# A hybrid encoder trunk on one core: ten up projections of the gated MLP by seven products, and the sums for them formed a block ahead

## The chip, the cores and the metric

The kernel runs on one core of a Trainium2 chip. Its engines are TensorE (PE in the profile, with PEld for its weight loads), VectorE (DVE), ScalarE (ACT), GpSimd (POOL) and SyncE (SP, which here only issues transfers). The metric is the device time of one execution in microseconds. The profile comes from one execution, and its durations are those of that execution.

## The reference, cut to what matters

The trunk has two layers over 512 tokens of width 1024. Each layer mixes tokens (differential attention in layer 0, gated linear attention in layer 1, cross-attention beside both) and then runs a gated MLP with a causal convolution of width 3. Only the MLP is touched by the change:

```python
D_MODEL, SEQ, DEPTH, D_FF, CONV_WIDTH = 1024, 512, 2, 2816, 3

def conv_ffn(h, w_up, conv_w, conv_b, w_down):
    u = h @ w_up                       # 512 x 1024 by 1024 x 5632
    c = lax.conv_general_dilated(u, conv_w[:, None, :], window_strides=(1,),
                                 padding=[(CONV_WIDTH - 1, 0)],
                                 dimension_numbers=('NWC', 'WIO', 'NWC'),
                                 feature_group_count=u.shape[-1]) + conv_b
    a, g = jnp.split(c, 2, axis=-1)
    return (jax.nn.silu(g) * a) @ w_down   # 512 x 2816 by 2816 x 1024

for i in range(DEPTH):
    ...
    h = rms_norm(x, ffn_norm[i])
    x = x + conv_ffn(h, w_up[i], conv_w[i], conv_b[i], w_down[i])
```

## The kernel before

**Products.** Everything is computed transposed: features on the 128 partitions, the 512 tokens along a row. fp32 factors are split into a high and a low part (`fp32r`), and each product is three matmuls: high by high, high by low, low by high. Weights arrive in blocks of 1024 columns (`raw`, three buffers, all on SP's queue); ACT casts a block to `whi` and DVE subtracts to get `wlo` (`split_weights`, L254 to L258; six buffers each, `WB`). The tokens' parts are `xsh` and `xsl`, one pair of tiles for each of the eight K tiles of 128.

**The MLP** is `ffn`. The 22 feature tiles of `D_FF` are done in three passes of 4, 4 and 3 groups q of 256 features (`HALVES`: q = 0 to 3, 4 to 7, 8 to 10). For each q there are two *up pieces*, `ua` (linear half) and `ug` (gate half), each with 256 columns of `w_up` in two blocks. A piece gives two PSUM banks of 128 x 512, n = 0 and 1, each by 24 matmuls of 512 columns (`up`, `product`, L387 to L389). The order on TensorE is written out by hand: ua n=0, ug n=0, ua n=1, ug n=1. Banks go round the eight of `TURNS`. After each bank, `conv` scales it on DVE (L1165), ACT writes the first tap into `cvo` (L1167), and DVE adds the two shifted taps (L1168, L1169). ACT applies Silu to the gate half (L1333), DVE multiplies (L1334), and `parts_of` splits the result into the tiles `mid` (L1190 on ACT, L1191 on DVE).

**Down by seven products.** After the up pieces of a pass come four *down pieces* of 256 output columns. Most (`dn`) already use a scheme of Strassen's kind: for a pair of K tiles, 2 x 2 blocks of weights times 2 x 2 blocks of data (tokens 0 to 255 are `left`, 256 to 511 `right`) cost seven products of 256 columns instead of eight. For that POOL forms four sums of each weight block's quarters (`combined`, L287 to L290, tile `wsum`), and four sums of each pair of `mid` tiles are formed by `combine` (L1198 to L1201, tile `tsum`; on POOL, but on DVE for a pass's last q). TensorE's rows are then L1247, and `decode` puts the seven results together (L1258 to L1266). Layer 0's last pass (`dw`) is plain: of each two columns, the first two groups q = 8 and 9 come first for both, q = 10 after that.

**What sets the order.** TensorE runs in program order. DVE, ACT and POOL run the order that a scheduler made from the program, each then strictly in turn. `weights` decides how far ahead blocks are split; `ahead` issues the next raw loads. Down, `refill` and `release` count the split blocks that are live (a `dn` block takes two of the six buffers).

## Time and profile before

| what | value |
|---|---|
| median of three runs | 1149.71 us (1149.57 to 1151.2) |
| the profiled execution | 1150.36 us |
| its span, first to last instruction | 1148.5 us |
| matmuls of layer 0's MLP, up of pass 1, 2, 3 begin | about 241, 368.50, 495.88 us |
| down of pass 1, 2, 3 begins | 328.19, 455.57, 561.20 us |
| layer 1's, up of pass 2 and 3 begins | 920.23, 1047.61 us |

Times in the views count from the span's start. A row of a group view names line, engine, operation, result and sources and the shape, with its count; then the busy time, the mean of one in ns, and the idle time ahead of it with what ended it. A row of the timeline starts with start and duration. A row of a table of stretches starts with the stretch and its length, and has the busy time and the count of PE, PEld, DVE, ACT and POOL, then the granted clock, the share of the transfer engines and GB/s. A row of the chain has the start, the time, and the engine with what it worked on.

### The profile page before, as it was taken

Reading aid. Unit: us, or ns where it says so; the run is one execution under the profiler, and the core shown is the slowest. Engines: PE = TensorE matmul, PEld = TensorE weight load, DVE = VectorE, ACT = ScalarE, POOL = GpSimd, SP = SyncE. Lnnn points to the kernel's source line nnn. Section 1 sums busy time; section 2 is a strip of 40 time slices with the busy share of each in tenths; the row PEclk is TensorE's granted clock in tenths of the full one; section 3 lists DMA queues with packets and bytes.
Section 4 is the critical chain, followed back from the end, with each engine's and each line's share of the span. In section 5 each row is a group of like instructions: output and inputs, shape, how many; then the busy total and the mean of one; then the engine's idle time right before and its main releaser. Section 6 shows DMA issues by size and latency. Waiting matters only on the chain.

```text
span 1148.5 us, 16655 instructions
## 1 busy us (share of the span) xinstructions
PE 1142.7 (99%) x6311; PEld 985.1 (86%) x6311; DVE 871.2 (76%) x1455; ACT 592.0 (52%) x1032; POOL 193.2 (17%) x230
## 2 busy tenths in 40 slices
PE   9999999999999999999999999999999999999998
PEld 7888888888899888988888888988888988899887
DVE  8576778688789677977677637777887977797777
ACT  6676686555454354434457634535644444453442
POOL 0000000001543125500000000000135403360340
PEclk9999999999999999999999999999999999999999
DMA  9522242133214322343252220333241342234212
GB/s 293 173 83 84 78 142 74 58 109 110 92 57 146 111 77 80 96 144 100 69 182 70 100 94 12 101 125 119 74 126 40 127 149 74 61 91 143 92 46 102
DMA packets 39662, 117.83 MB, mean 103 GB/s; under 512 B 4767, under 2 KB 7256, under 8 KB 39582
## 3 DMA queue, kind: packets, MB, share of 16 engines
q1 hardware_dynamic: 39150, 116.37, 31.8%
q8 instruction: 50, 0.82, 0.3%
q10 hardware_dynamic: 432, 0.39, 0.1%
q14 instruction: 30, 0.25, 0.1%
HBM read 112.54 MB, written 4.21 MB: 102 GB/s over the span
## 4 chain that ended last, share of the span: by engine, by line
PE 99%; DMA 0%; DVE 0%; ACT 0%; issue 0%
PE ps_mm L365 6%; PE ps_mm L367 6%; PE ps_mm L366 6%; PE ps_mm L387 6%; PE ps_mm L388 6%; PE ps_mm L389 6%; PE ps_lg L1247 5%; PE ps_sm L388 5%; PE ps_sm L389 5%; PE ps_sm L387 5%; PE ps_mm L1247 4%; PE ps_tp L388 4%; PE ps_lg L388 4%; PE ps_tp L387 4%; PE ps_lg L387 4%; PE ps_tp L389 4%
## 5 line engine op out<-in xcount | busy, mean ns | idle before, releaser
L258 DVE TENSOR_TENSOR wlo<-raw,whi 128x1024 fp32r<-128x1024 f32 (+4 forms) x174 | 194.2, 1127 | 77.0 <-ACT whi L255 76.4
L255 ACT CAST whi<-raw 128x1024 fp32r<-128x1024 f32 (+4 forms) x174 | 168.0, 976 | 124.2 <-PE ps_sm L388 29.8
L365 PE MATMUL ps_mm<-whi,xsh 128*128 128x512 f32 (+2 forms) x328 | 126.2, 385 | 0.0
L367 PE MATMUL ps_mm<-whi,xsl 128*128 128x512 f32 (+2 forms) x328 | 123.0, 375 | 0.0
L366 PE MATMUL ps_mm<-wlo,xsh 128*128 128x512 f32 (+2 forms) x328 | 122.8, 374 | 0.0
L387 PE MATMUL ps_mm<-xsh,whi 128*128 128x512 f32 x278 | 109.3, 393 | 0.0
L388 PE MATMUL ps_mm<-xsl,whi 128*128 128x512 f32 x278 | 108.4, 390 | 0.0
L389 PE MATMUL ps_mm<-xsh,wlo 128*128 128x512 f32 x278 | 108.2, 389 | 0.0
L387 PE MATMUL ps_sm<-xsh,whi 128*128 128x512 f32 x218 | 84.8, 389 | 0.0
L388 PE MATMUL ps_sm<-xsl,whi 128*128 128x512 f32 x218 | 84.8, 389 | 0.0
L389 PE MATMUL ps_sm<-xsh,wlo 128*128 128x512 f32 x218 | 84.8, 389 | 0.0
L365 PEld LDWEIGHTS ps_mm<-whi,xsh 128*128 128x128 f32 x328 | 61.7, 188 | 11.4 <-issue 1.0
L367 PEld LDWEIGHTS ps_mm<-whi,xsl 128*128 128x128 f32 x328 | 61.7, 188 | 11.3
L366 PEld LDWEIGHTS ps_mm<-wlo,xsh 128*128 128x128 f32 x328 | 61.8, 188 | 10.1
L387 PE MATMUL ps_lg<-xsh,whi 128*128 128x512 f32 x160 | 62.2, 389 | 0.0
L388 PE MATMUL ps_lg<-xsl,whi 128*128 128x512 f32 x160 | 62.2, 389 | 0.0
L389 PE MATMUL ps_lg<-xsh,wlo 128*128 128x512 f32 x160 | 62.2, 389 | 0.0
L387 PE MATMUL ps_tp<-xsh,whi 128*128 128x512 f32 x160 | 62.2, 389 | 0.0
L388 PE MATMUL ps_tp<-xsl,whi 128*128 128x512 f32 x160 | 62.2, 389 | 0.0
L389 PE MATMUL ps_tp<-xsh,wlo 128*128 128x512 f32 x160 | 62.2, 389 | 0.0
L389 PEld LDWEIGHTS ps_mm<-xsh,wlo 128*128 128x128 f32 x278 | 52.2, 188 | 11.0
L387 PEld LDWEIGHTS ps_mm<-xsh,whi 128*128 128x128 f32 x278 | 52.2, 188 | 10.8 <-issue 0.3
(382 smaller groups left out, 2835.4 us busy)
## 6 DMA issues: line engine op xcount, KB each, us to landing
raw<-in_wpack_dram SPq DMA_DIRECT2D x178, 512.0 KB, 3.5
xt<-in_x_t_dram SPq DMA_DIRECT2D x15, 256.0 KB, 5.2
raw<-in_wpack_dram SPq DMA_DIRECT2D x15, 256.0 KB, 3.1
raw<-in_wpack_dram SPq DMA_DIRECT2D x8, 384.0 KB, 3.0
xres<-xt SPq DMA_DIRECT2D x8, 256.0 KB, 3.2
xt<-xres SPq DMA_DIRECT2D x8, 256.0 KB, 5.8
out_dram<-xt SPq DMA_DIRECT2D x7, 256.0 KB, 2.0
bt<-bias_d SPq DMA_DIRECT2D x6, 256.0 KB, 4.1
```

The costliest lines, as they stand in the source:

```text
L255: ins = A.copy(hi[:, c], raw[:, c])
L258: V.tensor_sub(lo[:, c], raw[:, c], hi[:, c].bitcast(F32))
L365: mm(p, sh[k][:, blk(b)], hi, start=k == 0, stop=False)
L366: mm(p, sh[k][:, blk(b)], lo, start=False, stop=False)
L367: mm(p, sl[k][:, blk(b)], hi, start=False, stop=k == KT - 1)
L387: mm(p, hi[:, blk(n)], bh, start=i == first, stop=False)
L388: mm(p, hi[:, blk(n)], bl, start=False, stop=False)
L389: mm(p, lo[:, blk(n)], bh, start=False, stop=i == last)
L1247: mm(banks[c][b][:, h], w, v, start=b not in seen[c], stop=m == nq - 1 and t == 2 and i in close)
```

## The change

Ten up pieces, the list `SEVEN`, go over to seven products: `ua` of q = 5, 6, 8 and 9 in both layers, and in layer 0 also `ug` of q = 9 and `ua` of q = 10. Such a piece takes its K tiles in the order 6, 7, 4, 5, 0, 1, 2, 3. The pair (6, 7) stays plain, 12 matmuls of 512 columns; each other pair becomes 21 of 256 (`up_by_seven`). The piece holds four banks and gives both n at once, so both stand ahead of the gate half; one ACT copy and six DVE additions put them together before `conv`.

The tokens' side needs four sums for each of the three pairs, formed once a layer in pass 1 (`token_sums`, at `SUMS_AT`): ACT scales two tiles, POOL makes four sums, ACT and DVE split them into `vsh` and `vsl`. The weights' side needs `block_sums` on POOL for each block, of 128 columns for the first block of a piece and 256 for the second.

The sums of a block are now put down when the block is next to be split (in `ahead`), before the other work that comes between, and POOL keeps the program's order. POOL's sums of `mid` use the same tile `wsum` (two buffers), `tsum` is gone, and their splitting is put behind the third convolution that follows (`later`, `behind`). DVE's sums of `mid` use `cvo` tiles. `begin`, `refill` and `release` now count live blocks in the up products too, and up and down take banks from one round of `TURNS`. The program is built with a smaller scratch for descriptors.

```diff
-                piece(("ua", l, q), "w_up", l, K8, (256 * q, 256 * q + 256))
-                piece(("ug", l, q), "w_up", l, K8, (DFF + 256 * q, DFF + 256 * q + 256))
+                for key, c in ((("ua", l, q), 256 * q), (("ug", l, q), DFF + 256 * q)):
+                    piece(key, "w_up", l, (6, 7, 4, 5, 0, 1, 2, 3) if key in SEVEN else K8, (c, c + 256))
...
+SEVEN = [("ua", l, q) for l in range(2) for q in (5, 6, 8, 9)] + [("ug", 0, 9), ("ua", 0, 10)]
+SUMS_AT = {1:(4,5),2:(0,1),3:(2,3)}
...
+        i = order[done[0]][0] if done[0] < len(order) else None
+        if i is not None and by_seven(i) and done[0] not in summed:
+            summed[done[0]] = block_sums(raw_q[0], order[done[0]][1], int(plan[i][0][0] != "dn" and first_of[i] == done[0]))
...
+    def block_sums(raw, n, plain):
         pairs = n // 2
+        js, wsum = pairs - plain, sum_tile()
+        r = raw[:, :512 * pairs].rearrange("p (j i c) -> p j i c", j=pairs, i=4)
+        a12, a22, a11, a21 = (r[:, plain:, i] for i in range(4))
+        sv = wsum[:, :512 * js].rearrange("p (i j c) -> p i j c", i=4, j=js)
+        s1, s2, s3, s4 = (sv[:, i] for i in range(4))
+        g_sums((("add", s1, a21, a22), ("sub", s3, a11, a21), ("sub", s2, s1, a11), ("sub", s4, a12, s2)))
+        return wsum
+
+    def combined(raw, wsum, n, plain):
+        pairs = n // 2
...
+        if plain:
+            c = slice(0, 512 * plain + 384)
+            split_weights(c, raw, h0, l0)
+        else:
+            A.copy(full(h0)[:, :, :3], r[:, :, :3])
+            V.tensor_sub(full(l0)[:, :, :3], r[:, :, :3], full(h0)[:, :, :3].bitcast(F32))
+        m = slice(0, 512 * js)
         A.copy(h1[:, m], wsum[:, m])
         V.tensor_sub(l1[:, m], wsum[:, m], h1[:, m].bitcast(F32))
...
+    def by_seven(i):
+        return plan[i][0][0] == "dn" or plan[i][0] in SEVEN
+
+    def sum_tile():
+        return sum_pool[0].tile([128, WTILE], F32, name="wsum", bufs=2)
...
-        if plan[i][0][0] == "dn":
-            made[i] += combined(raw, n)
+        if by_seven(i):
+            made[i] += combined(raw, summed.pop(done[0] - 1), n, int(plan[i][0][0] != "dn" and not made[i]))
...
-        if i + 1 < len(plan) and plan[i + 1][0][0] in ("dn", "dw"):
-            limit = first_of[i + 1] + 1
...
+        def take(n):
+            nb[0] += n
+            return [bank(TURNS[i % 8]) for i in range(nb[0] - n, nb[0])]
+
+        def refill():
+            nonlocal live
+            while done[0] < min(len(order), first_of[min(used[0] + 2, len(plan))]) and live + sizes[done[0]] <= WB:
+                live += sizes[done[0]]
+                make_block()
+
+        def begin(key):
+            nonlocal live
+            assert plan[used[0]][0] == key, (plan[used[0]][0], key)
+            used[0] += 1
+            refill()
+            return used[0] - 1
+
+        def whole_piece(i):
+            nonlocal live
+            while done[0] < first_of[i + 1]:
+                live += sizes[done[0]]
+                make_block()
+            assert live <= WB
+            return made[i]
...
+        def release(i, n, all_of_it=False):
+            nonlocal live
+            live -= n
+            if all_of_it:
+                made[i] = None
...
+        def up(i, n):
+            p, = take(1)
+            product(p, whole_piece(i), n, tokens)
+            if n == 1:
+                release(i, 2, True)
...
+        def up_by_seven(i):
+            b, seen = take(4), set()
+            where = [(2, left), (0, left), (0, right), (1, left), (3, right), (2, right), (3, left)]
+            for m, ks in enumerate(((6, 7), (4, 5), (0, 1), (2, 3))):
+                while len(made) <= i or len(made[i]) <= m:
+                    refill()
+                part = made[i][m]
+                if m == 0:
+                    for n in range(2):
+                        product(b[n], part, n, [tokens[k] for k in ks], range(2), 99)
+                else:
+                    for r in steps:
+                        c, h = where[r]
+                        (hi, lo), (vh, vl) = part[r], sums_of[ks][r]
+                        for t, (w, v) in enumerate(((hi, vh), (hi, vl), (lo, vh))):
+                            mm(b[c][:, h], w, v, start=c > 1 and c not in seen, stop=m == 3 and t == 2 and r in (2, 5, 6, 3))
+                            seen.add(c)
+                if m % 2:
+                    release(i, 2, m == 3)
+            u, w = ctile(), ctile()
+            A.copy(u[:, left], b[2][:, left])
+            V.tensor_add(w[:, right], u[:, left], b[2][:, right])
+            V.tensor_add(u[:, right], w[:, right], b[3][:, right])
+            V.tensor_add(w[:, left], w[:, right], b[3][:, left])
+            V.tensor_add(w[:, right], u[:, right], b[3][:, left])
+            V.tensor_add(b[0], b[0], u)
+            V.tensor_add(b[1], b[1], w)
+            return b[:2]
...
+            first = A.activation(c, p, AF.Identity, scale=cv[l][:, 2, j:j + 1], bias=cv[l][:, 3, j:j + 1])
...
+            final = V.scalar_tensor_tensor(c[:, 2:], p[:, :S - 2], cv[l][:, 0, j:j + 1], c[:, 2:], op0=ALU.mult, op1=ALU.add)
+            if later:
+                convs[0] += 1
+                if convs[0] == 3:
+                    convs[0] = 0
+                    behind(first, final)
...
-        def combine(b2, b1, bh, bl, fh, fl, E):
-            t = pool.tile([128, 2 * S], F32, name="tsum", bufs=1)
+        def combine(b2, b1, bh, bl, fh, fl, E, parts):
+            t = [ctile(), ctile()] if E is V else [sum_tile()]
             q = [blk(i, 256) for i in range(4)]
...
-            h, lo = (pool.tile([128, 2 * S], F32R, name="mid2", bufs=9) for _ in range(2))
-            for c in ((blk(0, S), blk(1, S)) if E is V else (blk(0, 2 * S),)):
...
+        def mid_sums(c2, ops, E):
+            h, lo = (pool.tile([128, 2 * S], F32R, name="mid2", bufs=8) for _ in range(2))
+
...
+                    if E is V:
+                        parts_of(x, h[:, c], lo[:, c])
+                    else:
+                        later.append((x, h[:, c], lo[:, c]))
...
+        def behind(*ins):
+            with ExitStack() as stack:
+                for i in ins:
+                    stack.enter_context(tc.issue_after(i.ins))
+                while later:
+                    parts_of(*later.pop(0))
+
+        def scaled(k):
+            t = ctile()
+            A.activation(t, xT[k], AF.Copy, scale=c_ffn(l, k))
+            return t
+
+        def token_sums(ks):
+            (bh, bl), (fh, fl) = (tokens[k] for k in ks)
+            tiles = [split_tiles(pool, "vs", 12) for _ in range(2)]
+
+            def parts(t):
+                for i, (hi, lo) in enumerate(tiles):
+                    parts_of(t[0][:, blk(i, S)], hi, lo)
+            combine(scaled(ks[0]), scaled(ks[1]), None, None, None, None, G, parts)
+            h, lo = ([t[i][:, c] for t in tiles for c in (left, right)] for i in range(2))
+            sums_of[ks] = operands(h, lo, bh, bl, fh[:, left], fl[:, left])
...
-                wa = weights(("ua", l, q))
-                wg, c2, ops = None, [], []
...
+                def half(key, n, j):
+                    if n == 0:
+                        at[key] = begin((key, l, q))
+                        if (key, l, q) in SEVEN:
+                            cs[key] = [conv(p, j + i) for i, p in enumerate(up_by_seven(at[key]))]
+                    if key in cs:
+                        return lambda: cs[key][n]
+                    p = up(at[key], n)
+                    return lambda: conv(p, j + n)
+
...
-                    ca = conv(ua, 2 * q + n)
-                    cg = conv(ug, 22 + 2 * q + n)
+                    cn, cg = ua(), ug()
...
+                        parts_of(cn[:, left], *ops[-2:])
+                    if 2 * q + n in SUMS_AT:
+                        token_sums(SUMS_AT[2 * q + n])
...
-                    mids.append(combine(*c2, *ops, V if q == base + nq - 1 else ADD))
+                    mids.append(mid_sums(c2, ops, V if end else G))
```

**TensorE in layer 0's pass 3, `ua` of q = 8.** Numbers behind names are those of buffers; `xsh_2564` and `xsh_2588` are K tiles 4 and 5. Before, this pair's part of the bank for n = 0:

```order
L387 MATMUL ps_mm_5030<-xsh_2564,whi_4904 128x512
L388 MATMUL ps_mm_5030<-xsl_2565,whi_4904 128x512
L389 MATMUL ps_mm_5030<-xsh_2564,wlo_4905 128x512
L387 MATMUL ps_mm_5030<-xsh_2588,whi_4904 128x512
L388 MATMUL ps_mm_5030<-xsl_2589,whi_4904 128x512
L389 MATMUL ps_mm_5030<-xsh_2588,wlo_4905 128x512
```

and now the first four of the seven products of the same pair, both n together:

```order
L1233 MATMUL ps_lg_5218<-xsh_2564,whi_5068 128x256
L1233 MATMUL ps_lg_5218<-xsl_2565,whi_5068 128x256
L1233 MATMUL ps_lg_5218<-xsh_2564,wlo_5069 128x256
L1233 MATMUL ps_lg_5218<-xsh_2564,whi_5070 128x256
L1233 MATMUL ps_lg_5218<-xsl_2565,whi_5070 128x256
L1233 MATMUL ps_lg_5218<-xsh_2564,wlo_5071 128x256
L1233 MATMUL ps_tp_5220<-xsh_2588,whi_5068 128x256
L1233 MATMUL ps_tp_5220<-xsl_2589,whi_5068 128x256
L1233 MATMUL ps_tp_5220<-xsh_2588,wlo_5069 128x256
L1233 MATMUL ps_tp_5220<-vsh_2845,whi_5070 128x256
L1233 MATMUL ps_tp_5220<-vsl_2846,whi_5070 128x256
L1233 MATMUL ps_tp_5220<-vsh_2845,wlo_5071 128x256
```

Six matmuls of 512 columns (and six more for n = 1, a half later) have become 21 of 256, with the sums `vsh_2845` of the tokens and `whi_5070` of the weights among the factors and three banks in place of one.

**DVE in the same pass, around the pieces of q = 9.** Before, the first half's two banks of q = 9 (`ps_lg_5186` linear, `ps_lg_5223` gate) are each scaled and convolved as they come:

```order
L1165 TENSOR_TENSOR ps_lg_5186<-ps_lg_5186,rB_2659 128x512
L1191 TENSOR_TENSOR mid_5171<-cvo_5159,mid_5170 128x512
L1168 SCALAR_TENSOR_TENSOR cvo_5249<-ps_lg_5186,cv0_81,cvo_5249 128x511
L1169 SCALAR_TENSOR_TENSOR cvo_5249<-ps_lg_5186,cv0_81,cvo_5249 128x510
L1165 TENSOR_TENSOR ps_lg_5223<-ps_lg_5223,rB_2659 128x512
L1168 SCALAR_TENSOR_TENSOR cvo_5254<-ps_lg_5223,cv0_81,cvo_5254 128x511
L1169 SCALAR_TENSOR_TENSOR cvo_5254<-ps_lg_5223,cv0_81,cvo_5254 128x510
L258 TENSOR_TENSOR wlo_5331<-raw_5184,whi_5330 128x1024
L1334 TENSOR_TENSOR cvo_5249<-cvo_5249,cvo_5254 128x512
```

and now, at the gate piece `ug` of q = 9 by seven products (banks `ps_mm_5563` and `5564` for products, `ps_tp_5561` and `5562` for the result):

```order
L1240 TENSOR_TENSOR cvo_5662<-cvo_5663,ps_mm_5564 128x256
L260 TENSOR_TENSOR wlo_5651<-raw_5478,whi_5650 128x1024
L260 TENSOR_TENSOR wlo_5657<-raw_5535,whi_5656 128x1024
L1241 TENSOR_TENSOR cvo_5663<-cvo_5663,ps_mm_5564 128x256
L1243 TENSOR_TENSOR ps_tp_5561<-ps_tp_5561,cvo_5662 128x512
L1242 TENSOR_TENSOR cvo_5663<-cvo_5662,ps_mm_5564 128x256
L1248 TENSOR_TENSOR ps_tp_5561<-ps_tp_5561,rB_2659 128x512
L1244 TENSOR_TENSOR ps_tp_5562<-ps_tp_5562,cvo_5663 128x512
L260 TENSOR_TENSOR wlo_5731<-raw_5606,whi_5730 128x1024
L1251 SCALAR_TENSOR_TENSOR cvo_5672<-ps_tp_5561,cv0_81,cvo_5672 128x511
L1248 TENSOR_TENSOR ps_tp_5562<-ps_tp_5562,rB_2659 128x512
L1252 SCALAR_TENSOR_TENSOR cvo_5672<-ps_tp_5561,cv0_81,cvo_5672 128x510
```

Ahead of the two shifted taps (L1251, L1252) of the first result bank now stand additions from the product banks, the two result banks' additions (L1243, L1244) and three splits of weights (L260).

**POOL in layer 0's pass 2.** Before, the sums of two groups of `mid` follow each other, then comes a block of the down product's weights:

```order
L1198 TENSOR_TENSOR tsum_4003<-cvo_3989 128x256
L1200 TENSOR_TENSOR tsum_4003<-cvo_3923,cvo_3989 128x256
L1199 TENSOR_TENSOR tsum_4003<-cvo_3923,tsum_4003 128x256
L1201 TENSOR_TENSOR tsum_4003<-cvo_3923,tsum_4003 128x256
L1198 TENSOR_TENSOR tsum_4167<-cvo_4153 128x256
L1200 TENSOR_TENSOR tsum_4167<-cvo_4087,cvo_4153 128x256
L1199 TENSOR_TENSOR tsum_4167<-cvo_4087,tsum_4167 128x256
L287 TENSOR_TENSOR wsum_4381<-raw_4223 128x256
```

and now, in the same pass:

```order
L285 TENSOR_TENSOR wsum_4070<-raw_4031 128x128 x2
L285 TENSOR_TENSOR wsum_4070<-wsum_4070,raw_4031 128x128
L285 TENSOR_TENSOR wsum_4070<-raw_4031,wsum_4070 128x128
L1287 TENSOR_TENSOR wsum_4092<-cvo_4076 128x256
L1287 TENSOR_TENSOR wsum_4092<-cvo_3983,wsum_4092 128x256
L1287 TENSOR_TENSOR wsum_4092<-cvo_3983,cvo_4076 128x256
L1287 TENSOR_TENSOR wsum_4092<-cvo_3983,wsum_4092 128x256
L285 TENSOR_TENSOR wsum_4144<-raw_4062 128x256 x2
L285 TENSOR_TENSOR wsum_4144<-wsum_4144,raw_4062 128x256
L285 TENSOR_TENSOR wsum_4144<-raw_4062,wsum_4144 128x256
L1287 TENSOR_TENSOR wsum_4307<-cvo_4216 128x256
L1287 TENSOR_TENSOR wsum_4307<-cvo_4211,wsum_4307 128x256
```

The sums of the up pieces' blocks (L285, from `raw`) now stand between those of the groups of `mid` (L1287), all in `wsum`.

134 lines of the change are left out of this document (55 added, 79 removed).

## The prediction

> **What bounds the kernel now.** I read the page's busy shares, the chain of work that ended last and the view of TensorE's waits first, in that order.
>
> ```profile
> span 1148.5 us, 16655 instructions
> PE 1142.7 (99%) x6311; PEld 985.1 (86%) x6311; DVE 871.2 (76%) x1455; ACT 592.0 (52%) x1032; POOL 193.2 (17%) x230
> PE 99%; DMA 0%; DVE 0%; ACT 0%; issue 0%
> ...
> PE ps_tp L492 <- PEq L1399: 0.8, 1, 0.8
> PE ps_mm L566 <- DVE whi L528: 0.4, 1, 0.4
> PE ps_mm L566 <- ACT xsh L345: 0.2, 1, 0.2
> ```
>
> TensorE is busy for 99% of the span and is 99% of the chain. The three waits are all it has, 1.4 us together, all in the opening lines of the program. So the kernel is a queue of matmuls with no gap in it: taking matmul time away shortens it by just that, as long as nothing behind the queue comes late. The second busiest is VectorE (DVE). How near it is to its limit is read by stage (PE, weight load, DVE, ACT, POOL busy and count in each):
>
> ```profile
> 241.00:328.19 87.19, 87.19 (x387) 72.18 (x385) 65.98 (x86) 41.96 (x56) 20.61 (x24) 1.00 0.30 97
> 368.50:455.57 87.07, 87.07 (x387) 72.08 (x386) 64.86 (x85) 38.21 (x50) 21.20 (x26) 1.00 0.30 94
> 455.57:495.88 40.31, 40.31 (x338) 40.31 (x336) 37.54 (x50) 18.87 (x25) 18.68 (x19) 1.00 0.36 113
> 495.88:561.20 65.32, 65.32 (x291) 54.07 (x290) 47.52 (x63) 26.43 (x35) 0.42 (x1) 1.00 0.30 96
> 561.20:593.83 32.63, 32.63 (x146) 27.02 (x145) 19.85 (x27) 16.42 (x23) 2.15 (x5) 1.00 0.43 138
> 1047.61:1112.92 65.31, 65.31 (x291) 54.06 (x289) 48.05 (x65) 27.71 (x37) 17.77 (x24) 1.00 0.27 86
> ```
>
> These are layer 0's up products of pass 1 and pass 2, down of pass 2, up and down of pass 3, and layer 1's up of pass 3. DVE has 17 to 22 us free in each up stage and under 3 us in the down stage. The granted clock is 1.00 throughout.
>
> **What TensorE saves.** The next rows are a 512-wide half of an up piece, then the chain in a down stage (256-wide), then 256-wide matmuls of another projection.
>
> ```profile
> 506.79 0.39 PE L387 MATMUL ps_sm<-xsh,whi 128*128 128x512 f32 x1
> 507.01 0.39 PE L388 MATMUL ps_sm<-xsl,whi 128*128 128x512 f32 x1
> ...
> 512.23 0.39 PE L387 MATMUL ps_sm<-xsh,whi 128*128 128x512 f32 x1
> ...
> 350.66 1.08 PE ps_mm L1247 x9
> 353.18 1.08 PE ps_mm L1247 x9
> ...
> 729.67 0.28 PE L365 MATMUL ps_mm<-whi,xsh 128*128 128x256 f32 x1
> 730.03 0.28 PE L365 MATMUL ps_mm<-whi,xsh 128*128 128x256 f32 x1
> ```
>
> A half is 24 matmuls, and the next half starts 512.23 − 506.79 = 5.44 us later: 0.2267 us each. Nine 256-wide ones take 1.08 us, and the round of 21 repeats after 353.18 − 350.66 = 2.52 us: 0.120 us each; outside the down stage three take 0.36, the same. A pair of K tiles of an up piece costs 12 × 0.2267 = 2.72 us plain and 21 × 0.120 = 2.52 by seven products: 0.20 saved. Three of a piece's four pairs change, so a piece goes from 10.88 to 10.28, and ten pieces (four in each layer, two more in layer 0's pass 3) save 10 × 0.60 = **6.0 us**. Of what a 256-wide matmul may cost in its new place the rows bound it: in the down stage weight loads fill 40.31 of 40.31 us and the step is still 0.120, which is the denser case, so I take 0.120 (a step of 0.1295 would eat the saving).
>
> The Trainium skill ("TensorE: Matmul & The Clock Gate", section "Back-to-back issue gap") puts the gap at N/2.4 + 2.5 ns, that is 216 and 109 ns; by it a pair would save 0.30 and the change 8.9 us. The rows above disagree with it on both widths, and the sum goes by the rows.
>
> **What the others get, and what hides it.** Here are the groups that price it (busy, mean ns, idle before), and three rows of DVE's timeline.
>
> ```profile
> L258 DVE TENSOR_TENSOR wlo<-raw,whi 128x1024 fp32r<-128x1024 f32 x143 | 172.7, 1219 | 70.7 <-ACT whi L255 70.2
> L258 DVE TENSOR_TENSOR wlo<-raw,whi 128x768 fp32r<-128x768 f32 x8 | 7.5, 952 | 1.0 <-ACT whi L255 1.0
> L292 DVE TENSOR_TENSOR wlo<-raw,whi 128x768 fp32r<-128x768 f32 x35 | 37.4, 1068 | 0.0
> L295 DVE TENSOR_TENSOR wlo<-wsum,whi 128x1024 fp32r<-128x1024 f32 x35 | 47.9, 1368 | 1.5 <-ACT whi L294 1.3
> L258 DVE TENSOR_TENSOR wlo<-raw,whi 128x512 fp32r<-128x512 f32 x12 | 8.2, 681 | 2.5 <-ACT whi L255 2.5
> L1261 DVE TENSOR_TENSOR cvo<-cvo,ps_lg 128x256 f32<-128x256 f32 x10 | 4.2, 421 | 0.8
> L1263 DVE TENSOR_TENSOR xt<-xt,ps_lg 128x512 f32<-128x512 f32 x10 | 6.8, 679 | 0.0
> L1191 DVE TENSOR_TENSOR mid<-cvo,mid 128x512 fp32r<-128x512 f32 x28 | 19.7, 704 | 2.4 <-ACT mid L1190 2.1
> L287 POOL TENSOR_TENSOR wsum<-raw 128x256 f32<-128x256 f32 x35 | 30.2, 862 | 112.3 <-DVE wlo L295 58.3 <-DMA raw<-in_wpack_dram 34.1 <-issue 19.9
> ...
> 536.19 0.68 DVE L1191 TENSOR_TENSOR mid<-cvo,mid 128x512 fp32r<-128x512 f32 x1
> 536.79 0.74 DVE L1168 SCALAR_TENSOR_TENSOR cvo<-ps_tp,cv,cvo 128x511 f32<-128x511 f32 x1
> ...
> 552.05 0.75 DVE L1168 SCALAR_TENSOR_TENSOR cvo<-ps_mm,cv,cvo 128x511 f32<-128x511 f32 x1 [0.85 <-ACT cvo L1167]
> ```
>
> Decoding a piece: four 256-wide adds and two 512-wide ones, 4 × 0.42 + 2 × 0.68 = 3.0 us of DVE, and one ACT copy. Splitting its weights: before two times 1.22; now 896 columns (1.08, between the 768 and 1024 rows), 512 (0.68), 768 (1.07) and 1024 (1.37): 4.2, so 1.8 more. That makes 4.8, less about 0.08 for each of the eight more instructions, by which a DVE instruction's end overlaps the next's start (the 0.68 us one at 536.19 is followed at 536.79): **4.2 us of DVE per piece**. The token sums of pass 1 cost two 512-wide splits a pair, 2 × 0.70 = 1.4, three pairs a layer: 4.2. POOL gets four sums for every block of a piece, 4 × 0.86 = 3.4 us at most, and 24 token sums; ACT, 52% busy, gets the copies and casts that go with them. No transfer is added, and the weight loads keep their number on SP's queue.
>
> Covers. Pass 1: 4.2 into 21.2 free. Pass 2: two pieces, 8.4 into 22.2. Layer 1's pass 3: two pieces, 8.4 into 17.3. All of it lies beside matmuls, and I cost it at nothing; without that cover it would be 4 to 8 us a stage. **Layer 0's pass 3 is the exception**: four pieces bring 16.8, and the stage's free time is 65.32 − 47.52 = 17.8 less the 2.4 that TensorE now saves there: 15.4. DVE is over-full by 1.4 us, and work has to run on into the down products. How late that may be, and how a transition looks now:
>
> ```profile
> 563.72 0.75 DVE L1169 SCALAR_TENSOR_TENSOR cvo<-ps_sm,cv,cvo 128x510 f32<-128x510 f32 x1
> 566.60 0.69 DVE L1191 TENSOR_TENSOR mid<-cvo,mid 128x512 fp32r<-128x512 f32 x1 [0.69 <-ACT mid L1190]
> ...
> 572.07 0.39 PE L387 MATMUL ps_lg<-mid,whi 128*128 128x512 f32 x1
> ...
> 464.99 1.28 DVE L1191 TENSOR_TENSOR mid<-tsum,mid 128x512 fp32r<-128x512 f32 x2
> 469.82 1.49 DVE L292 TENSOR_TENSOR wlo<-raw,whi 128x768 fp32r<-128x768 f32 x1
> ```
>
> Before, the last `mid` of pass 3 is there at 566.60 + 0.69 = 567.3, and TensorE reads that group at 572.07: 4.8 us early, since two columns of the down product run first on older groups. Walking the new DVE order with the durations above, the last split ends 1 to 1.5 us ahead of its reader. One place before is tighter: the up gate half of q = 10 goes into the bank that the gate piece of q = 9 leaves, one seven-product piece (10.28 us) after that piece's end; DVE has four 256-wide adds (1.5), four 512-wide passes on PSUM (2.4), two shifted multiply-adds (1.5) and three 1024-wide splits (3.4) ahead of it, and 0.85 for ACT's first tap: 9.65. It comes 0.6 us early. At pass 2's transition the sums of the last group are split at 464.99 + 1.28 = 466.3, 10.7 us into the down stage; they are read from 102 matmuls, 12.24 us, on. Now they come a few tenths to 1.5 us later, which leaves 0.9 to 1.8 us for the groups as they are read.
>
> So the stalls are between 0 and, where these margins are gone by DVE rows that stretch beside POOL (1068 for 952, 1368 for 1219, and once 1.49), some 2.5 us in layer 0's pass 3 and 1 at each of the four up-to-down transitions of passes 2 and 3: 0 to 6 us. I take 0.5, nearer the lower end, because the walk with mean durations shows no wait. The smaller scratch for descriptors has no row; what lies around the span is 1150.36 − 1148.5 = 1.9 us, so it can give or take little more, and I take 0.
>
> **Sum.** 1150.36 − 6.0 + 0.5 = 1144.9 in the terms of the profiled execution, whose time is 0.65 above the runs' median of 1149.71: **1144.2 us**. About 0.2% (2.3 us) is the least that a measurement here tells from no change.
>
> **Rivals.**
> 1. *The margins go in layer 0's pass 3 and at the transitions.* The 0.6 us margin at q = 10 and the 0.9 at the transitions are smaller than one stretched DVE instruction (1.49 for 0.95). For it: DVE is over-full there. Against: POOL's sums are few where DVE is fullest, and a late DVE catches up in the down stage of pass 3 (19.85 of 32.63). Price: 2 to 5 us back, 1146 to 1149.
> 2. *DVE becomes the bound at every seven-product piece; slower.* A piece's two result banks are used again 10.88 + 2.72 = 13.6 us after its end (by the next seven-product piece's second pair). Until then DVE has the decode (3.0), two multiplies (1.2), four shifted ones (3.0) and four splits (about 4.2): 11.4. It decides once DVE's instructions run 20% longer than their rows, 13.7; the stretched rows show 12% on the mean and 57% at worst. At 30% they take 14.8, a wait of 1.2 us for each of ten pieces, 12 us for a gain of 6: about 1156. For it: POOL's adds, which stretch DVE, now stand in the up stages of all seven-product pieces. Against: only the splits stretch in the rows, not what works on PSUM.
> 3. *POOL's adds shut DVE out.* The sums of a piece's two blocks, up to 6.9 us, would then add wholly to DVE's 11.4: 18.3 against 13.6, 4.7 us for each of ten pieces, near 1190. Against: the split's mean beside POOL is 0.12 to 0.15 longer, not an addition's 0.86. The Trainium skill ("SBUF — State Buffer", on the shared port pair) has such a rule: the one that comes second is blocked for the whole of the other's instruction. Of the rows here only the 1.49 looks so, and the mean doesn't.
> 4. *The change's 256-wide matmuls do not keep 0.120 in their new place*, since every product now goes to another bank with another operand: at 0.127 a pair saves 0.05, 1.6 us in all, 1148, no change that can be told. Against: the down stage's products do the same at 0.120.
>
> **Chances.** The forecast (1143.2 to 1146) 0.60; rival 1 0.20, half of it still faster by over 0.2% and half within; rival 2 0.13; rival 3 0.03; rival 4 0.04. Faster 0.60 + 0.10 = 0.70, within 0.2% 0.10 + 0.04 = 0.14, slower 0.13 + 0.03 = 0.16. The range runs from 1143.0 (all of the saving on the median is 1143.7, and a row's rounding is a few tenths) over rival 1 and 4 to 1152, just past the bound of slower; it leaves out most of rivals 2 and 3, 0.15.
>
> **What would show it.** The up stages of pass 2 (87.07) shorter by 1.2 us each, layer 0's pass 3 (65.32) by 2.4, layer 1's (65.31) by 1.2, pass 1 and the down stages as before. TensorE waits still under 2.5 us, and if there are any, in ps_tp or on `mid` of layer 0's pass 3, released by DVE. DVE about 50 us busier (10 × 4.2 + 2 × 4.2), POOL by 60 to 90 (20 × 3.4 and 24 × 0.8 at most). Waits of 0.5 us or more on a bank or a weight in every seven-product piece would prove me wrong, and so would L1260-like adds well over 0.42 or a step other than 0.120 between its matmuls.

## The result, and the profile after

The changed kernel takes 1151.91 us (median of 20 runs, 1150.34 to 1153.07), beside 1149.85 for the kernel before on the same chip (20 runs): a ratio of 1.0016, with a 95% interval of 1.0010 to 1.0023. That lies within the bound of 0.2%, and on the slow side, where 0.5% faster was forecast. The profiled execution took 1151.93. Here are its span and busy times, and the chain that ended last.

```profile
span 1150.1 us, 17576 instructions
PE 1140.5 (99%) x6581; PEld 994.6 (86%) x6581; DVE 939.9 (82%) x1547; ACT 618.8 (54%) x1086; POOL 282.6 (25%) x334
PE 75%; DVE 16%; ACT 4%; issue 2%; POOL 1%; DMA 0%; ACTq 0%; POOLq 0%; DVEq 0%
```

TensorE's waits (sum, times, longest):

```profile
PE ps_sm L1359 <- DVE mid L1279: 2.7, 4, 0.8
PE ps_tp L1359 <- DVE mid L1279: 2.5, 4, 0.8
PE ps_tp L512 <- PEq L1515: 0.8, 1, 0.8
```

TensorE was 99% of the chain and is now 75%. "99% busy" hides that: the busy share rounds away 9.6 us, where it was 5.8 before. Two new rows stand in the waits, both in the down products, both for a `mid` part that DVE has not split yet. Eight waits, 5.2 us. Where they stand shows in the table of stages (columns as in the prediction's); the first two rows are layer 0's down of pass 1 and up of pass 2, then its down of pass 2, up and down of pass 3, then layer 1's down of pass 1, up and down of pass 2, up of pass 3 and the last down.

```profile
328.70:370.42 41.72, 40.83 (x337) 40.42 (x336) 38.55 (x49) 18.62 (x24) 22.34 (x22) 1.00 0.35 106
370.42:456.33 85.91, 85.91 (x441) 73.70 (x439) 75.12 (x101) 40.94 (x55) 30.75 (x38) 1.00 0.32 97
456.33:499.10 42.77, 41.07 (x337) 40.46 (x336) 40.59 (x51) 18.29 (x26) 30.25 (x31) 1.00 0.30 88
499.10:562.09 62.99, 62.99 (x399) 57.28 (x397) 58.79 (x88) 30.77 (x43) 20.22 (x25) 1.00 0.34 105
562.09:594.72 32.63, 32.63 (x145) 27.04 (x144) 24.67 (x35) 18.07 (x26) 2.15 (x5) 1.00 0.49 153
880.82:923.86 43.04, 41.07 (x337) 40.46 (x336) 39.94 (x50) 19.21 (x26) 24.03 (x25) 1.00 0.33 101
923.86:1009.77 85.91, 85.91 (x441) 73.69 (x439) 75.68 (x103) 40.68 (x55) 32.19 (x39) 1.00 0.32 97
1009.77:1051.24 41.47, 40.71 (x337) 40.41 (x336) 39.30 (x49) 18.24 (x25) 28.91 (x30) 1.00 0.29 92
1051.24:1115.39 64.15, 64.15 (x345) 55.67 (x343) 57.44 (x81) 31.83 (x42) 23.54 (x28) 1.00 0.31 98
1115.39:1138.44 23.05, 22.93 (x190) 22.73 (x189) 22.09 (x35) 10.76 (x17) 9.33 (x13) 1.00 0.23 69
```

The up stages gave what was taken out: 87.07 to 85.91 in each layer, 65.32 to 62.99, 65.31 to 64.15, that is 1.16 + 1.16 + 2.33 + 1.16 = **5.8 us saved**. The down stages gave it back. They were 40.31 before in passes 1 and 2 (22.67 for the last one): 1.41 + 2.46 + 2.73 + 1.16 + 0.38 = **8.1 us lost**. (That is more than the 5.2 of the waits. Each costs some 0.26 more than the view lists: a matmul that waited 0.76 us starts 1.04 after its predecessor, 342.05 to 343.09, in place of 0.12, and the next one 0.22 behind it. Two waits of 0.3 us are not in the view at all.) Net 2.3; outside these stages the span is 0.7 shorter: 0.5 longer ahead of the first of them and 1.2 shorter behind the last. The profiled execution of the kernel before was a long one there: its span of 1148.5 us is above the 1147.1 to 1148.3 of its 57 executions beside the runs below. Layer 0's pass 3 (62.99 and 32.63) has no wait.

### The profile page after: what moved, and what is told of

The parts are those of the page before. It is cut to its first block, busy times and chain, and to the rows that moved or that the text cites. A ratio compares the mean times of both kernels' runs of the same rounds, so it can differ in the third digit from the quotient of the medians.

```text
span 1150.1 us, 17576 instructions
## 1 busy us (share of the span) xinstructions
PE 1140.5 (99%) x6581; PEld 994.6 (86%) x6581; DVE 939.9 (82%) x1547; ACT 618.8 (54%) x1086; POOL 282.6 (25%) x334
## 4 chain that ended last, share of the span: by engine, by line
PE 75%; DVE 16%; ACT 4%; issue 2%; POOL 1%; DMA 0%; ACTq 0%; POOLq 0%; DVEq 0%
PE ps_mm L385 6%; PE ps_mm L387 6%; PE ps_mm L386 6%; PE ps_mm L407 5%; PE ps_mm L408 5%; PE ps_mm L409 5%; PE ps_lg L1359 3%; PE ps_mm L1359 3%; PE ps_tp L224 3%; PE ps_sm L408 3%; PE ps_sm L407 3%; DVE mid L1279 3%; PE ps_tp L1359 2%; PE ps_sm L409 2%; PE ps_lg L1233 2%; PE ps_sm L1359 2%
## 5 line engine op out<-in xcount | busy, mean ns | idle before, releaser
L260 DVE TENSOR_TENSOR wlo<-raw,whi 128x1024 fp32r<-128x1024 f32 (+5 forms) x164 | 185.9, 1145 | 70.0 <-ACT whi L257 69.1
L257 ACT CAST whi<-raw 128x1024 fp32r<-128x1024 f32 (+5 forms) x164 | 155.7, 965 | 103.1 <-PE ps_mm L408 23.1
L285 POOL TENSOR_TENSOR wsum<-raw 128x256 f32<-128x256 f32 (+1 forms) x116 | 92.7, 820 | 128.9 <-DMA raw<-in_wpack_dram 65.1
L1287 POOL TENSOR_TENSOR wsum<-cvo 128x256 f32<-128x256 f32 x40 | 34.0, 850 | 225.0 <-DVE cvo L1448 139.2
L312 DVE TENSOR_TENSOR wlo<-wsum,whi 128x1024 fp32r<-128x1024 f32 (+1 forms) x58 | 75.2, 1297 | 9.2 <-ACT whi L311 9.2
L311 ACT CAST whi<-wsum 128x1024 fp32r<-128x1024 f32 (+1 forms) x58 | 55.3, 953 | 41.9 <-POOL wsum L285 39.8
L408 PE MATMUL ps_sm<-xsl,whi 128*128 128x512 f32 x190 | 74.0, 389 | 0.0
L407 PE MATMUL ps_sm<-xsh,whi 128*128 128x512 f32 x190 | 74.0, 389 | 0.0
L409 PE MATMUL ps_sm<-xsh,wlo 128*128 128x512 f32 x190 | 73.9, 389 | 0.0
L387 PEld LDWEIGHTS ps_mm<-whi,xsl 128*128 128x128 f32 x328 | 61.7, 188 | 11.3
L407 PEld LDWEIGHTS ps_mm<-xsh,whi 128*128 128x128 f32 x294 | 55.2, 188 | 11.3 <-issue 0.3
L408 PEld LDWEIGHTS ps_mm<-xsl,whi 128*128 128x128 f32 x294 | 55.3, 188 | 11.2 <-DVE xsl L366 0.4
```

Source lines behind the costliest of these rows:

```text
L257: ins = A.copy(hi[:, c], raw[:, c])
L260: V.tensor_sub(lo[:, c], raw[:, c], hi[:, c].bitcast(F32))
L285: tc.keep_in_program_order(getattr(G, "tensor_" + op)(o, x, y))
L311: A.copy(h1[:, m], wsum[:, m])
L312: V.tensor_sub(l1[:, m], wsum[:, m], h1[:, m].bitcast(F32))
L387: mm(p, sl[k][:, blk(b)], hi, start=False, stop=k == KT - 1)
```

## What DVE does at such a transition

The first rows are DVE's, at the end of layer 0's pass 1 before the change (its down stage begins at 328.19). The split of the last group's sums is one row of two instructions.

```profile
338.66 1.28 DVE L1191 TENSOR_TENSOR mid<-tsum,mid 128x512 fp32r<-128x512 f32 x2
339.86 1.21 DVE L295 TENSOR_TENSOR wlo<-wsum,whi 128x1024 fp32r<-128x1024 f32 x1
```

The same place after the change (down begins at 328.70):

```profile
328.85 1.76 DVE L1279 TENSOR_TENSOR mid<-wsum,mid 128x1024 fp32r<-128x1024 f32 x1
...
332.33 1.36 DVE L312 TENSOR_TENSOR wlo<-wsum,whi 128x1024 fp32r<-128x1024 f32 x1 [1.11 <-ACT whi L311]
...
340.61 0.68 DVE L1279 TENSOR_TENSOR mid<-cvo,mid 128x512 fp32r<-128x512 f32 x1
341.21 1.22 DVE L312 TENSOR_TENSOR wlo<-wsum,whi 128x1024 fp32r<-128x1024 f32 x1
342.35 0.68 DVE L1279 TENSOR_TENSOR mid<-cvo,mid 128x512 fp32r<-128x512 f32 x1
```

Counted from the start of the down stage, TensorE reads the first half of these sums from 12.24 us on and the second from 12.96. Before, both were there at 338.66 + 1.28 − 328.19 = 11.75. Now the first ends at 340.61 + 0.68 − 328.70 = 12.59 and the second at 14.33. Two things are new. A split of a down block's weights, L312 with 1.22 us, stands *between* the halves. And what comes ahead is late: DVE idles 1.11 us for ACT's cast of a block's sums, which ACT, in strict order, had stood waiting for while POOL made them:

```profile
326.67 1.44 POOL L285 TENSOR_TENSOR wsum<-raw 128x256 f32<-128x256 f32 x2 [4.39 <-DVE wlo L312]
328.07 1.46 POOL L285 TENSOR_TENSOR wsum<-wsum,raw 128x256 f32<-128x256 f32 x1
...
331.24 1.05 ACT L311 CAST whi<-wsum 128x1024 fp32r<-128x1024 f32 x1 [3.56 <-POOL wsum L285]
332.20 0.77 ACT L1250 ACTIVATE cvo<-ps_tp,cv 128x512 f32<-128x512 f32 x1
```

POOL had to wait for a `wsum` buffer. There are two, for the sums of blocks and now of `mid` as well; one holds a group's sums of `mid` until their split, put behind the third convolution, runs (the row at 328.85). So the sums of the blocks had the other buffer alone, and the wait of 4.39 us ended when L312 had split the block's sums that were in it. Behind ACT's waiting cast stands the first tap of the last half (L1250), so the last convolution is late too.

That gives three theories: *order* (what stands between the last two splits), *buffer* (the late split holds `wsum`), *load* (DVE, or POOL's contention with it, is simply too much near the transitions).

## The experiments

Twelve kernels ran, each beside the kernel before. In their expectations "the deferred split", also where it is called that of the token sums, is the split of a group's sums of `mid` over token halves (the 1024-wide L1278 and L1279 from `wsum`). Only the "token sums" left in or out at e3, e8 and e10 are the new `token_sums` at `SUMS_AT`. Here are the stalls that the change and eight of the runs left in the down stages, from the starts of the matmuls in the profiled executions (us; the time is the median). The profiled execution of e2 was 1.3 us above its median, that of e3 0.8 above, that of e5 1.1 below; the others of the table lie within 0.5. The kernel before had medians of 1149.49 to 1149.88 beside these runs.

| kernel | L0 p1 | L0 p2 | L1 p1 | L1 p2 | L1 p3 | sum | time |
|---|---|---|---|---|---|---|---|
| the change | 1.4 | 2.5 | 2.7 | 1.2 | 0.4 | 8.1 | 1151.91 |
| e1 split at once | 5.4 | 1.5 | 3.5 | 0.9 | 0.6 | 11.9 | 1155.51 |
| e2 fewer blocks ahead | 1.4 | 3.6 | 2.8 | 1.2 | 0.4 | 9.3 | 1151.93 |
| e3 no pieces, no token sums | 0.7 | 0.7 | 0.7 | 0.7 | 0.4 | 3.2 | 1152.77 |
| e8 no pieces, token sums in | 1.4 | 0.7 | 2.8 | 0.7 | 0.3 | 5.9 | 1155.86 |
| e5 sums first | 0 | 0.4 | 1.2 | 0 | 0.4 | 2.0 | 1146.35 |
| e9 = e3, sums first | 0 | 0 | 0 | 0 | 0.4 | 0.4 | 1149.89 |
| e6 split behind the 2nd convolution | 0 | 0 | 0 | 0 | 0 | 0 | 1143.56 |
| e10 = e8, split behind the 2nd | 0 | 0 | 0 | 0 | 0 | 0 | 1150.11 |

### e1 to e4: the first look

e1 drops the deferral:

```diff
-                        later.append((x, h[:, c], lo[:, c]))
+                        parts_of(x, h[:, c], lo[:, c])
```

> The changed kernel, but POOL's sums of mid are split at once instead of behind the third convolution that follows. Theory 'deferral' (the deferred 1024-wide split of the last group but one falls into the last group's chain on DVE, holds one of the two wsum buffers, so that POOL's block sums and the ACT cast behind them come late, and it parts the last two splits): the waits at the up-to-down transitions, 8.1 us in all in the changed kernel's trace, go to under 1.5; time 1144 to 1146. Theory 'load' (the seven-product pieces fill DVE): transitions as in the changed kernel, 1151 to 1152. Theory 'look-ahead' (the blocks of the down product are split too early, since the old bound on it is gone): no change either, 1151 to 1152.

Measured: 1155.51, ratio 1.0046 (1.0033 to 1.0058), worse than the change and outside every theory's range. Splitting at once makes ACT wait in order for POOL's chain of sums, and DVE, behind it, idles 2.50 us ahead of its own part (ACT's timeline):

```profile
323.17 1.05 ACT L1278 CAST mid<-wsum 128x1024 fp32r<-128x1024 f32 x1 [2.68 <-POOL wsum L1287]
```

So the deferral has a use. In e1 no other split stands between the last two at the transitions of passes 1 and 2; DVE is late as a whole. What was left open is whether the deferral is too long.

e2 puts back a bound on how many blocks are prepared ahead of a down stage:

```diff
+            limit = first_of[min(used[0] + 2, len(plan))]
+            if used[0] < len(plan) and plan[used[0]][0][0] in ("dn", "dw") and plan[used[0] - 1][0][0] == "ug":
+                limit = first_of[used[0]] + 1
```

> The changed kernel with the old bound put back: while the last up piece of a pass runs, only one block of the down product is split ahead. Theory 'look-ahead': 1144 to 1147. Theory 'deferral': the deferred split stays where it is, 1150.5 to 1152.5. Theory 'load': 1151 to 1152.

Measured: 1151.93, ratio 1.0018 (1.0009 to 1.0027); stalls at the same places, none smaller (the 3.6 in layer 0's pass 2 is that of the slower profiled execution). The number of blocks ahead is not the cause.

e3 takes the ten pieces and the token sums out and keeps everything else of the change:

```diff
+SEVEN = []
+SUMS_AT = {}
```

> The changed kernel with an empty list of seven-product up pieces and no token sums: its new order, buffers and block sums ahead, but the arithmetic on TensorE of the kernel before. Theory 'deferral': the waits at the transitions stay (5 to 8 us) and nothing is saved, 1155 to 1158. Theory 'load': no waits, 1149 to 1151. Theory 'look-ahead': waits stay, 1155 to 1158.

Measured: 1152.77, ratio 1.0022 (1.0013 to 1.0032), so 3 us slower than before with the same matmuls, and between the ranges of the theories. The rest of the change costs by itself: 0.7 us at each of four transitions, and every time at the second half of the last sums. DVE there, from the end of the first half on (the down stage begins at 329.10):

```profile
340.89 1.21 DVE L312 TENSOR_TENSOR wlo<-wsum,whi 128x1024 fp32r<-128x1024 f32 x1
342.03 0.68 DVE L1279 TENSOR_TENSOR mid<-cvo,mid 128x512 fp32r<-128x512 f32 x1
```

It ends 342.03 + 0.68 − 329.10 = 13.61 into the stage, for a reader at 12.96.

e4 goes from the other side: the kernel before, with the split deferred behind the third convolution, in its own tile `tsum`.

```diff
-                parts_of(t[:, c], h[:, c], lo[:, c])
+                if E is V:
+                    parts_of(t[:, c], h[:, c], lo[:, c])
+                else:
+                    later.append((t[:, c], h[:, c], lo[:, c]))
```

> The kernel before with one edit: POOL's sums of mid, still in their own tile tsum, are split behind the third convolution that follows. Theory 'deferral' in its form 'the split itself in the last chain is enough': waits of 0.5 to 1.5 us at each of five transitions, 1152 to 1156. In its form 'the shared wsum buffer is needed for it': under 1 us in all, 1149.5 to 1151. Theories 'load' and 'look-ahead': 1149.5 to 1150.5.

Measured: 1149.97, ratio 1.0000 (0.9991 to 1.0009), no wait in the down stages. A late split costs nothing here, where it holds no buffer that somebody else needs. Yet DVE has the order of the change at the end, with a down block's split (L295) between the halves (down from 328.35):

```profile
337.80 1.21 DVE L295 TENSOR_TENSOR wlo<-wsum,whi 128x1024 fp32r<-128x1024 f32 x1
338.93 0.68 DVE L1196 TENSOR_TENSOR mid<-tsum,mid 128x512 fp32r<-128x512 f32 x1
```

The second half ends 338.93 + 0.68 − 328.35 = 11.26 into the stage, 1.7 us ahead of its reader. So this order alone costs nothing where DVE comes in time.

### e5 and e9: the sums first

The first down block's release, from which the splits L309 and L312 of the next block follow, is issued behind the split of the last sums:

```diff
-                    release(first + c, 1 if whole[c] else 2, m == nq - 1)
+                    with ExitStack() as stack:
+                        if c == 0 and not whole[0]:
+                            stack.enter_context(tc.issue_after(ends[0].ins))
+                        release(first + c, 1 if whole[c] else 2, m == nq - 1)
```

> The changed kernel, in whose up-to-down transitions the release of the first down block (its splits on VectorE, L309 and L312) is issued behind the split of the last product's sums, where in the changed kernel the 1.22 us of L312 stands between the two halves of that split. Arithmetic and instructions are the same. If the stalls at the start of the down stages come from what stands between the splits (theory 'tail order'), the four transitions of passes 1 and 2 lose most of their second stall: about 1.1 us less in each of the two in pass 1 and 0.7 to 1.2 us less in each of pass 2, about 2 to 4 us in all: 1148 to 1150. If VectorE arrives late as a whole (theory 'load'), the first half's stall stays and the sum falls by less than 1.5 us: 1150.5 to 1151.5. If GpSimd's contention alone does it, no change: 1151.9, within 0.1%.

Measured: 1146.35, ratio 0.9970 (0.9960 to 0.9981): the gain was 5.6 us on the change, more than any theory gave. DVE's timeline at layer 0's pass 1 (down from 328.19), then ACT's, with the cast there:

```profile
339.66 1.29 DVE L1279 TENSOR_TENSOR mid<-cvo,mid 128x512 fp32r<-128x512 f32 x2 [0.23 <-ACT mid L1278]
...
341.74 1.22 DVE L312 TENSOR_TENSOR wlo<-wsum,whi 128x1024 fp32r<-128x1024 f32 x1
```

```profile
330.74 1.05 ACT L311 CAST whi<-wsum 128x1024 fp32r<-128x1024 f32 x1 [3.54 <-POOL wsum L285]
```

The halves are neighbours and end 339.66 + 1.29 − 328.19 = 12.76 into the stage, 0.2 us ahead of the reader, although ACT still waits 3.54 for POOL. DVE is as late as before the edit; only what it does first differs. Where it is later still, in layer 1's pass 1, 1.2 us remain. The edit puts L309 behind the last sums too, so the first half also gains.

> The run without pieces and without token sums in the linear halves (e3: 3.2 us of stalls, all at the second half of the last sums' split), now with the first down block's release issued behind that split. TensorE's work is that of before plus nothing. Theory 'tail order': the stalls of the four transitions of passes 1 and 2 vanish, and of the 3.2 us only layer 1's pass 3, 0.4 us, stays: 1149.7 to 1150.2, no change against before. If these stalls came from lateness of VectorE as a whole or from the other buffers of the changed kernel: 1151.5 to 1152.8.

Measured: 1149.89, ratio 1.0001 (0.9991 to 1.0010). All of the stalls of e3 but the 0.4 of the last stage are the order of the last splits.

### e6, e7, e10: the split earlier

```diff
-                if convs[0] == 3:
+                if convs[0] == 2:
```

> The changed kernel with its deferred split of the token sums put behind the second convolution of the half instead of behind the third, so that the wsum buffer which holds those sums comes free earlier and GpSimd's sums for the next linear half, which waited 4.39 us in layer 0's pass 1, start earlier. Theory 'shared wsum buffers': ScalarE's cast that stood 3.56 us ahead of the last tap's product goes earlier, and the first stall of the pass-1 transitions shrinks; 1148 to 1150. Theory 'tail order': VectorE's order at the very end decides whatever the buffer does; gain only where the last two splits become neighbours, about 1 us a layer: 1149.5 to 1151. Theory 'load': the same work in another order, 1151 to 1152.

Measured: **1143.56**, ratio 0.9949 (0.9935 to 0.9962), better than each theory's number. TensorE's only wait is the 0.8 us of the opening lines, and the chain is TensorE's again:

```profile
PE 99%; DMA 0%; DVE 0%; issue 0%; SPq 0%; ACT 0%
```

The timelines of DVE, and then of POOL and ACT, at the transition of layer 0's pass 1 (down from 328.36):

```profile
322.04 1.22 DVE L1279 TENSOR_TENSOR mid<-wsum,mid 128x1024 fp32r<-128x1024 f32 x1
...
339.00 1.28 DVE L1279 TENSOR_TENSOR mid<-cvo,mid 128x512 fp32r<-128x512 f32 x2
340.21 1.21 DVE L312 TENSOR_TENSOR wlo<-wsum,whi 128x1024 fp32r<-128x1024 f32 x1
```

```profile
323.34 2.54 POOL L285 TENSOR_TENSOR wsum<-raw 128x256 f32<-128x256 f32 x2 [1.19 <-DVE mid L1279]
...
328.79 1.06 ACT L311 CAST whi<-wsum 128x1024 fp32r<-128x1024 f32 x1 [0.22 <-POOL wsum L285]
```

The split of the sums of `mid` stands at 322.04 in place of 328.85, 6.5 us sooner as counted from the down stage, and frees its `wsum`: POOL's next sums of a block start right behind it, after a wait of 1.19 us that this split ended, in place of 4.39. ACT waits 0.22 us for POOL in place of 3.56, and the last sums are whole 339.00 + 1.28 − 328.36 = 11.92 into the stage, in time for both readers. The order at the end changed with it: the scheduler no longer puts L312 between the halves. So this one number cures both lateness and order, and the run doesn't tell their shares apart.

> The last two edits together: the deferred split behind the second convolution, and the first down block's release behind the split of the last product's sums. If tail order and shared buffers each cause a part of the 8.1 us of stalls, the gains add up: 1145.5 to 1148. If one theory holds alone, this stands within 0.5 us of the better of the two. If VectorE is simply too loaded near the transitions, 1150 to 1152.

Measured: 1143.76, ratio 0.9946 (0.9934 to 0.9958), within 0.2 of e6. With the split earlier there is nothing left for the other edit.

> The changed kernel with all ten pieces of the up and gate products back to eight products (no block sums on VectorE, 0.60 us more TensorE each, 6.0 us in all) and with the token sums of the middle's splits left in the linear halves as the changed kernel has them, which nothing reads. This leaves TensorE's work of before and adds only the scheduling, the sums' buffers and their splits. Theory 'token sums cost pass 1': the stalls of the pass-1 transitions stay as in the changed kernel, 1.4 and 2.7 us, and those of pass 2 fall to 0.7 each: 1154 to 1156. Theory 'pieces load VectorE': all transitions fall to 0.7 as in the run without pieces or sums: 1152.5 to 1153.2.

Measured: 1155.86, ratio 1.0054 (1.0040 to 1.0067); 0.7 in pass 2 and the change's own stalls in pass 1. The token sums, the third user of POOL and `wsum`, are what makes pass 1 worse than e3 (DVE splits them from 271 to 298 us, 30 us ahead of the transition in layer 0, and no run shows on what path they act there); the pieces (1.8 us in layer 0's pass 2, 0.5 in layer 1's) what makes pass 2 worse.

> The run with eight products everywhere and the token sums left in (e8: 1155.9, 6.0 us of stalls), now with the deferred split behind the second convolution. Nothing reads the token sums. If the held wsum buffer is what the token sums cost, and the pieces have no part in it, the stalls vanish as they did with the pieces in place: 1149.5 to 1150.2, the time of before, and the difference to the run with the pieces and this edit (1143.6) is the ten pieces' 6.0 us alone. If the cure needed the pieces (another order on VectorE by chance): 1151.5 to 1155.

Measured: 1150.11, ratio 1.0003 (0.9994 to 1.0013), no stall. The cure does not need the pieces. The spans of this run and of e6, 1147.6 and 1141.6, differ by 6.0 us, and by nothing but the ten pieces.

### e11 and e12: how far it goes

e11 makes a block's sums when the block is split, not a block ahead, on top of e6:

```diff
-            made[i] += combined(raw, summed.pop(done[0] - 1), n, int(plan[i][0][0] != "dn" and not made[i]))
+            plain = int(plan[i][0][0] != "dn" and not made[i])
+            made[i] += combined(raw, block_sums(raw, n, plain), n, plain)
```

> The kernel with the deferred split behind the second convolution (1143.6), but with GpSimd's sums of a block's raw pieces issued when the block itself is split, as before the change, and not a block ahead. Theory 'a block ahead is needed': ScalarE's casts of the sums, which stand in order, wait for GpSimd's chain of 3 to 6 us at every seven-product block, so VectorE comes late at blocks and at transitions: over 1146, with waits on wlo. If the margins of the blocks cover it: 1143.5 to 1144.5, and the block ahead brings nothing.

Measured: 1170.34, ratio 1.0178 (1.0163 to 1.0193). 26.8 us hang on the block ahead, five stretches of half the clock included (the last section). ACT's largest group of waits (sum, times, longest); in e6 the same group is 35.4 us, 21 times, 2.9:

```profile
ACT whi L308 <- POOL wsum L282: 84.9, 36, 5.7
```

e12 adds two pieces to e6, in layer 1's pass 3:

```diff
-SEVEN = [("ua", l, q) for l in range(2) for q in (5, 6, 8, 9)] + [("ug", 0, 9), ("ua", 0, 10)]
+SEVEN = [("ua", l, q) for l in range(2) for q in (5, 6, 8, 9)] + [("ug", 0, 9), ("ua", 0, 10), ("ug", 1, 9), ("ua", 1, 10)]
```

> The kernel with the deferred split behind the second convolution (1143.6), with two more pieces by seven products: layer 1's pass 3, the gate piece of the second last group and the up piece of the last, as layer 0 has them. Each saves TensorE 0.60 us. If covers hold as in layer 0's pass 3: 1142.3 to 1142.6. If VectorE, with some 4.2 us more for each piece, runs out of cover in this shorter pass, stalls return at its transition: 1143.5 to 1147.

Measured: 1159.18, ratio 1.0082 (1.0067 to 1.0097): 15.6 us slower than e6, where TensorE was to save 1.2, and beyond both ranges. About 5 us of the loss lie in that up stage and 11 in the down stage behind it. DVE is busy for 56.9 of the 67.9 us of the up stage (in e6 58.2 of 64.1), so over the stage it is not full. TensorE's longest wait, 2.70 us at 1099.05, comes first, in the up stage, for a bank that DVE's second tap (L1252) had not left (its row stands in the last section): a wait on a bank of an up piece, as the second rival has it, at the place at q = 10 where the prediction found 0.6 us to spare in layer 0. The timelines of POOL, ACT and DVE at the end of layer 1's up of pass 3:

```profile
1106.26 0.74 POOL L1287 TENSOR_TENSOR wsum<-cvo,wsum 128x256 f32<-128x256 f32 x1
...
1108.33 0.46 POOL L285 TENSOR_TENSOR wsum<-raw,wsum 128x128 f32<-128x128 f32 x1
```

```profile
1108.83 0.62 ACT L311 CAST whi<-wsum 128x512 fp32r<-128x512 f32 x1 [4.55 <-PE ps_tp L408]
```

```profile
1109.48 0.69 DVE L312 TENSOR_TENSOR wlo<-wsum,whi 128x512 fp32r<-128x512 f32 x1 [3.53 <-ACT whi L311]
```

POOL makes the sums of a group of `mid` first (L1287) and the block's after them; ACT's cast waits for these. (The view names TensorE as the releaser, but POOL's last sum ends at 1108.33 + 0.46 = 1108.79, just ahead of the cast.) DVE idles 3.53 us in that order, and TensorE waits next. This reading comes from the trace; no run took it apart.

## Why the prediction was wrong

**The step that failed** is the one from the covers to the stalls: "All of it lies beside matmuls, and I cost it at nothing", and then "I take 0.5, nearer the lower end, because the walk with mean durations shows no wait", with 6 us as the most. (Its own terms, 2.5 and four times 1, make 6.5, or 5.5 with layer 0's pass 3 counted once.) Measured: 8.1. Three things were wrong in it.

*The place.* The worst was put in layer 0's pass 3, the one stage where DVE is over-full; it has no wait at all. DVE's added work was sized well: 58.79 us in the up stage and 24.67 in the down stage are 11.3 and 4.8 more than before, 16.1 of the 16.8 foreseen. More of it ran on than the 1.4 worked out, and the next stage took that. Pass 1 was left out of the bounds, because 21 us were free there. Its two transitions lost 4.1 us. Free time summed over a stage says nothing on whether one instruction is there at one moment.

*What the split's place holds.* The prediction counted the sums' durations, not the buffer. That the sums of `mid` moved to `wsum`, and that their split waits for a third convolution, were both in the diff; the walk took POOL's sums as there when wanted. e4 shows the late split harmless in a tile of its own, in the kernel before; e6 and e10 show its place to be the whole of the loss in the shared one. The changed kernel was not run with a tile of its own for these sums.

*The order at the end.* "Now they come a few tenths to 1.5 us later, which leaves 0.9 to 1.8 us" was said of layer 0's pass 2. (The figures ahead of it, 12.24 less 10.7, leave 1.5 before the change and so 0 to 1.2 after it.) It treated the last split as one instruction. Here is that place after the change (down from 456.33):

```profile
469.30 0.68 DVE L1279 TENSOR_TENSOR mid<-cvo,mid 128x512 fp32r<-128x512 f32 x1
469.90 1.21 DVE L312 TENSOR_TENSOR wlo<-wsum,whi 128x1024 fp32r<-128x1024 f32 x1
471.03 0.68 DVE L1279 TENSOR_TENSOR mid<-cvo,mid 128x512 fp32r<-128x512 f32 x1
```

The second half ends 471.03 + 0.68 − 456.33 = 15.4 us into the stage, 4.7 later than the 10.7 of before, with L312 between the halves. e3 and e9 price that at 2.8 us with nothing else changed (3.2 less 0.4). The order of the changed program shows it, and was not read at that place. The two causes overlap and don't add: e5 removes 6.2 us by the order alone (5.6 in the medians), e6 all 8.1. At most places the loss needs both. In e4 the order stands without lateness and nothing is lost, in e9 the lateness (DVE still idles 1.1 us for ACT's cast) without the order and only the 0.4 of the last stage is lost.

**Right:** the saving, 5.8 us by stages (6.0 in the spans of e10 and e6) against 6.0 forecast. With stalls at nothing, the sum's own terms give 1150.36 − 6.0 − 0.65 = 1143.7, and e6 has 1143.56: the prediction holds for the kernel in which its assumption is true.

In the sum, the term that failed is the stalls: 0.5 taken, 8.1 measured.

**Rivals.** The first named the transitions and had the mechanism half right, with "2 to 5 us back" and its first place wrong. The second, DVE as the bound at every piece, did not come: no wait stands on a bank or a weight of an up piece in the change. Nor did the third: e6 runs POOL 302.9 us, more than the change's 282.6, without a stall, so neither contention nor load as such is the cause. But "only the 1.49 looks so" read the rows too kindly. In the change POOL's 1.46 at 328.07 ends 0.68 us after DVE's split at 328.85 has begun, and that split takes 1.76 us, where the same split takes 1.22 in e6: single rows are held up much as the rival says, though TensorE does not wait for it in e6. The fourth falls with the stages' 0.58 us a piece. Of what was to show, DVE is 68.7 us busier, not 50: the pages give 7.7 from before to e3 (neither pieces nor token sums), 14.2 from e3 to e8 (the token sums, 8.4 foreseen) and 46.8 from e8 to the change (4.7 a piece, 4.2 foreseen). POOL is 89.4 busier, at the end of 60 to 90.

**What stays open:** why the scheduler puts L312 between the halves. It goes with the split's place: at the transitions of passes 1 and 2 a down block's split stands there in the change, e2, e3, e4 and e8, all with the split behind the third convolution, in e4 even in a tile of its own; it does not in the kernel before, e1, e6 and e10, with the split at once or behind the second. What ties the two was not tried.

## What to carry to other kernels

When an operand's split or copy is moved later, ask first what buffer it holds and who waits in order for that buffer; the distance has a best value (of the three tried here the second convolution: at once costs 12 us more, the third 8), and it is one number to try. At a change of stage, walk the order to the very last operand that the next stage reads, instruction by instruction, since spare time of a stage does not help there. And time work beside a full TensorE by deadlines: with all deadlines met, the plain sum of matmul times was right to 0.2 us.
